# Reads of a pair of score banks given precedence on VectorE and ScalarE in both mixers of a two-layer encoder trunk

## The chip, the cores and the metric

The kernel runs on one core of one Trainium2 chip. The metric is device time in microseconds (us) of one execution, the median of several. The engines are named as in the profile: PE is TensorE (matmuls; PEld its weight loads), DVE is VectorE, ACT is ScalarE, POOL is GpSimd, SP is SyncE, which issues the DMAs.

## The reference

Two layers over 1024 tokens of width 1024, all in float32. Layer 0 mixes tokens with two groups of heads side by side: eight heads of latent attention (MLA) and eight of stick-breaking attention. Layer 1 mixes them with sixteen heads of attention over a band of chunks with a learned bias. After each mixer comes a SwiGLU feed-forward part, around all of them RMS norms and residuals. Cut to the parts of the change:

```python
# MLA, per block of 128 queries
s_a = einsum(q_a[blk], k_a[:kend]) * scale_a
p_a = softmax(where(chunk_ok, s_a, -inf))
# stick-breaking, per block of 128 queries
z = einsum(q_b[blk], k_b[:kend]) * scale_b
log_keep = where(before, log_sigmoid(-z), 0)
log_between = cumsum(log_keep, reverse=True) - log_keep
w_b = where(before, exp(log_sigmoid(z) + log_between), 0)
# chunk band: own chunk and the 8 before it
p = softmax(where(valid, einsum(q, k_band) + bias, -inf))
```

## The kernel before

Every large matmul is made of three with float32 operands that are rounded to a shorter form and a rest: high by high, high by low, low by high (lines 287 to 289 in `mm3`). So each weight that comes from memory (`wr`) is split: `wh` is its rounded form, `wl` the rest, one instruction each of 128x512 (lines 250, 252 and 255 in `round_to` and `rest`). Which engine does a split is written out per weight. Activations are split in the same way (`u`, `c`).

PSUM, into which PE writes, is cut into three sets: two single banks `mm` for projections, two single banks `o` for outputs, and two *pairs* of banks `z`. A pair holds a tile of scores for two heads (128 x 2 x 512 at most). Whoever takes a pair waits until the one that had it two takes ago has been read. All attention goes through these two pairs:

- Stick-breaking (`sb_step`): for each tile of 128 keys by up to 512 queries and two heads, four matmuls give scores `z` (lines 901, 902); DVE clamps them into `a` (904), which frees the pair. ACT does Exp and Ln (905, 906), DVE a maximum (907), ACT and then DVE and POOL (one head each) split the result into `c` (911, 255). A later stage takes another pair and sums along the keys by matmuls with a triangle (923, 926, 928). ACT and DVE carry the last row on to the next tile (930, 931); DVE subtracts the sums from `a` (934), which frees that pair, and ACT does the exponential (935). The last stage multiplies with the values (838 in `weighted`).
- MLA: `mla_max` makes scores (1056) and takes row maxima `m` (1058) on DVE; they are gathered (1038) and transposed on PE (1040), and go negated into the queries (1042). `mla_attend` makes the scores again (1127 to 1129), ACT takes the exponential out of the pair (1130). `soft_step` divides by the sum (1095 to 1101).
- Band: `band_max` adds the bias and takes the maximum in one instruction per head (1185), `band_attend` adds the bias (1210) and takes the exponential (1211).

`step` runs the three stages of a tile with a distance of `LAG` = 2 tiles between them. `weave` mixes the attention of one pair of heads with *fill*: the projections of the next pair, which need only weights and so can run while attention waits. In the stick-breaking part fill is `sb_project` (the next heads' queries and keys) and values; with the last pair of heads, `prepare` (MLA's latent projections, their norms at 310 and 323 to 327, rotary embedding at 995 to 997).

What sets the order: inside the mixers a scheduler of the framework puts the instructions of each engine in a queue. It takes what is ready, by rank, and the rank is the place in the program. Once it is set, each engine works through its queue in order and waits at the first instruction that is not ready. The feed-forward parts are pinned to the order of the program.

## Time and profile before

| | us |
|---|---|
| three runs, median (lowest to highest) | 2587.18 (2587.08 to 2593.2) |
| the profiled execution | 2588.75 |
| its span, first to last instruction | 2586.6 |
| PE busy from 660 to 1340 us (feed-forward of layer 0, projections of layer 1) | 669.23 of 680 |
| PE busy from 1880 us on (end of layer 1) | 683.41 of 707 |

A row of the page or of a group names the line, the engine, the operation and its tiles with their shapes. Behind the bar stand the busy time, the mean duration of one in ns, and the idle time of the engine just before them with what ended it. A row of the waits names the waiting instruction, what it waited for, the total, the number of times and the longest.

### The profile page before, as it was taken

Reading aid. Unit: us, or ns where it says so; the run is one execution under the profiler, and the core shown is the slowest. Engines: PE = TensorE matmul, PEld = TensorE weight load, DVE = VectorE, ACT = ScalarE, POOL = GpSimd, SP = SyncE. Lnnn points to the kernel's source line nnn. Section 1 sums busy time; section 2 is a strip of 40 time slices with the busy share of each in tenths; the row PEclk is TensorE's granted clock in tenths of the full one; section 3 lists DMA queues with packets and bytes.
Section 4 is the critical chain, followed back from the end, with each engine's and each line's share of the span. In section 5 each row is a group of like instructions: output and inputs, shape, how many; then the busy total and the mean of one; then the engine's idle time right before and its main releaser. Section 6 shows DMA issues by size and latency. Waiting matters only on the chain.

```text
span 2586.6 us, 33550 instructions
## 1 busy us (share of the span) xinstructions
PE 2508.9 (97%) x11710; PEld 1935.2 (75%) x11710; DVE 1897.3 (73%) x3074; ACT 1168.5 (45%) x2028; POOL 515.5 (20%) x489
## 2 busy tenths in 40 slices
PE   7999998999999999999999999999999999999997
PEld 6766765557778888888878777776777888888886
DVE  6888887666787666677765777777778766667776
ACT  4677676444444344443352343334445443443324
POOL 3333324663000000000031333335300000000004
PEclk9999999999999999999999999999999999999999
DMA  4221100115524343475651222222543434447661
GB/s 139 62 64 54 54 17 29 31 58 163 171 90 151 122 147 133 144 265 193 235 181 54 88 74 83 77 70 90 176 166 102 163 106 142 143 138 261 212 227 70
DMA packets 179432, 319.70 MB, mean 124 GB/s; under 512 B 20544, under 2 KB 36800, under 8 KB 179264
## 3 DMA queue, kind: packets, MB, share of 16 engines
q1 hardware_dynamic: 179264, 317.56, 36.9%
q8 instruction: 93, 1.52, 0.2%
q14 instruction: 75, 0.61, 0.1%
HBM read 222.58 MB, written 84.41 MB: 119 GB/s over the span
## 4 chain that ended last, share of the span: by engine, by line
PE 72%; DVE 9%; DMA 2%; ACT 2%; issue 1%; POOL 0%; DVEq 0%; SPq 0%; POOLq 0%; ACTq 0%
PE z L74 24%; PE mm L74 12%; PE o L74 6%; PE mm L287 6%; PE mm L289 6%; PE mm L288 6%; PE o L838 4%; DVE u L74 2%; PE z L1208 2%; PE z L1182 1%; PE z L1209 1%; PE z L1095 1%; DVE u L310 1%; PE z L1127 1%; DMA wr<-in_w_down 1%
## 5 line engine op out<-in xcount | busy, mean ns | idle before, releaser
L74 PE MATMUL z<-u,wh 128*128 128x512 f32 x976 | 302.2, 390 | 6.4 <-DVE u L74 6.4
L74 PE MATMUL z<-u,vh 128*128 128x512 f32 x976 | 301.7, 390 | 2.8 <-DVE u L74 2.8
L287 PE MATMUL mm<-u,wh 128*128 128x512 f32 x720 | 291.6, 405 | 2.9 <-DVE c L996 1.8
L289 PE MATMUL mm<-u,wl 128*128 128x512 f32 x720 | 284.0, 394 | 0.0
L288 PE MATMUL mm<-u,wh 128*128 128x512 f32 x720 | 283.9, 394 | 0.0
L255 POOL TENSOR_TENSOR wl<-wr,wh 128x512 fp32r<-128x512 f32 (+2 forms) x95 | 122.8, 1297 | 804.3 <-ACT wh L250 732.9
L74 PE MATMUL mm<-u,wh 128*128 128x512 f32 x720 | 224.6, 393 | 3.7 <-ACT wh L74 3.7
L74 PEld LDWEIGHTS z<-u,wh 128*128 128x128 f32 x976 | 183.2, 188 | 47.2 <-DVE u L74 9.4
L74 PEld LDWEIGHTS z<-u,vh 128*128 128x128 f32 x976 | 182.9, 188 | 43.0 <-ACT u L74 4.4
L74 PE MATMUL z<-u,wl 128*128 128x512 f32 x488 | 190.0, 389 | 0.5 <-DVE wl L74 0.5
L74 PE MATMUL z<-u,vl 128*128 128x512 f32 x488 | 189.9, 389 | 0.0
L287 PEld LDWEIGHTS mm<-u,wh 128*128 128x128 f32 x720 | 135.5, 188 | 63.0 <-issue 39.0
L838 PE MATMUL o<-a,u 128*64 128x512 f32 (+3 forms) x768 | 169.6, 488 | 0.2 <-ACT a L1211 0.2
L74 PEld LDWEIGHTS mm<-u,wh 128*128 128x128 f32 x720 | 135.5, 189 | 34.8 <-ACT wh L74 5.6
L289 PEld LDWEIGHTS mm<-u,wl 128*128 128x128 f32 x720 | 135.5, 188 | 32.6 <-issue 5.4
L288 PEld LDWEIGHTS mm<-u,wh 128*128 128x128 f32 x720 | 135.8, 189 | 28.6 <-issue 5.7
L74 PE MATMUL mm<-u,vh 128*128 128x512 f32 x496 | 152.7, 389 | 0.0
L255 POOL TENSOR_TENSOR u<-wr,u 128x512 fp32r<-128x512 f32 x8 | 10.9, 1373 | 667.5 <-ACT u L250 667.5
L74 PE MATMUL mm<-u,wl 128*128 128x512 f32 x360 | 141.2, 392 | 0.7 <-DVE wl L74 0.5
L1211 ACT ACTIVATE a<-a 128x1024 f32<-128x1024 f32 (+3 forms) x96 | 70.5, 738 | 145.1 <-DVE a L1210 144.9
L74 ACT CAST vh<-vr 128x512 fp32r<-128x512 f32 (+1 forms) x166 | 95.9, 577 | 81.5 <-DVE vr L74 31.5
L1079 POOL TENSOR_TENSOR b<-b,a 128x512 f32<-128x512 f32 (+3 forms) x80 | 108.0, 1350 | 114.0 <-ACT a L1211 100.0
(249 smaller groups left out, 5937.7 us busy)
## 6 DMA issues: line engine op xcount, KB each, us to landing
u<-f_t SPq DMA_DIRECT2D x144, 256.0 KB, 5.0
vr<-in_w_up SPq DMA_DIRECT2D x88, 256.0 KB, 4.4
wr<-in_w_gate SPq DMA_DIRECT2D x88, 256.0 KB, 3.6
f_t<-x SPq DMA_DIRECT2D x72, 256.0 KB, 2.0
wr<-in_w_out SPq DMA_DIRECT2D x64, 256.0 KB, 3.0
f_t<-e SPq DMA_DIRECT2D x54, 256.0 KB, 3.6
ld<-f SPq DMA_DIRECT2D x54, 256.0 KB, 5.1
h<-u SPq DMA_DIRECT2D x48, 256.0 KB, 2.5
```

What stands on the lines that cost most here:

```text
L74: return lambda *a, **k: self.tc.keep_in_program_order(f(*a, **k))
L255: self.eng(eng).tensor_tensor(lo, src, hi.bitcast(F32), ALU.subtract)
L287: mm(out, wh, xh, start=first, stop=False, skip_group_check=onto)
L288: mm(out, wh, xl, start=False, stop=False, skip_group_check=onto)
L289: mm(out, wl, xh, start=False, stop=last, skip_group_check=onto)
L310: self.eng(eng).tensor_tensor(acc, acc, sq, ALU.add)
L838: self.nc.tensor.matmul(o[rh, cs], vt[j // 4][:, j % 4, rh], w[:, e, cs], start=first, stop=last)
L1079: self.eng("dve" if dest[2] else "pool").tensor_tensor(st["esum"][:, :, cs], old[:, :, cs], ex[:, :, cs], ALU.add)
L1095: nc.tensor.matmul(den[64 * e:64 * e + 64, :], self.ones[:, 0:64], esum[:, e, :], start=True, stop=True)
L1127: mm(z[:, e, cs], kth[0:kr, bs], qh[0:kr, cs], start=True, stop=False)
L1208: mm(z[:, e, cs], ks[e][kh][0][:, bs], qs[e][hf][0][:, cs], start=True, stop=False)
L1211: nc.scalar.activation(ex[:, :, cs], ex[:, :, cs], AF.Exp)
```

## The change

Seven instructions that read a pair of score banks (and the exponential behind the band's addition) are put in a block that raises their rank by 100 places. Nothing else is touched: each engine has the same instructions as before, in another order.

```diff
+URGENT = 100
...
+    def urgent(self):
+
+        return self.tc.high_priority(offset=URGENT)
...
             zc, t = self.tmp("a"), self.tmp("b")
-            nc.vector.tensor_scalar(zc[:, :, cs], z[:, :, cs], ZMAX, None, ALU.min)
+            with self.urgent():
+                nc.vector.tensor_scalar(zc[:, :, cs], z[:, :, cs], ZMAX, None, ALU.min)
...
             w = x["zc"]
-            nc.vector.tensor_tensor(w[:, :, cs], w[:, :, cs], b[:, :, cs], ALU.subtract)
+            with self.urgent():
+                nc.vector.tensor_tensor(w[:, :, cs], w[:, :, cs], b[:, :, cs], ALU.subtract)
...
-                nc.vector.reduce_max(m2[:, :, r, kh], z[:, :, :n], axis=AX.X)
+                with self.urgent():
+                    nc.vector.reduce_max(m2[:, :, r, kh], z[:, :, :n], axis=AX.X)
...
-                nc.scalar.activation(ex[:, :, cs], z[:, :, cs], AF.Exp, scale=96 ** -0.5)
+                with self.urgent():
+                    nc.scalar.activation(ex[:, :, cs], z[:, :, cs], AF.Exp, scale=96 ** -0.5)
...
-                for e in range(2):
-                    nc.vector.tensor_tensor_reduce(out=z[:, e, :n], in0=z[:, e, :n], in1=tq[:, e, y0:y0 + n],
-                                                   op0=ALU.add, op1=ALU.max, scale=1.0, scalar=-3.0e38,
-                                                   accum_out=m2[:, e, r, kh:kh + 1])
+                with self.urgent():
+                    for e in range(2):
+                        nc.vector.tensor_tensor_reduce(out=z[:, e, :n], in0=z[:, e, :n], in1=tq[:, e, y0:y0 + n],
+                                                       op0=ALU.add, op1=ALU.max, scale=1.0, scalar=-3.0e38,
+                                                       accum_out=m2[:, e, r, kh:kh + 1])
...
-                nc.vector.tensor_tensor(ex[:, :, cs], z[:, :, cs], tk[:, :, xs], ALU.add)
-                nc.scalar.activation(ex[:, :, cs], ex[:, :, cs], AF.Exp)
+                with self.urgent():
+                    nc.vector.tensor_tensor(ex[:, :, cs], z[:, :, cs], tk[:, :, xs], ALU.add)
+                    nc.scalar.activation(ex[:, :, cs], ex[:, :, cs], AF.Exp)
```

The seven are, by the line numbers of before, 904 and 934 (stick-breaking), 1058 and 1130 (MLA), 1185, 1210 and 1211 (band). Line numbers of the changed kernel are 1 to 11 higher. The prediction uses those of before. What moves in the queues is shown at three places. Tiles are named by a letter for their kind and a number that is theirs alone, in both kernels.

**The end of the third pair of heads in stick-breaking** (about 258 to 292 us of before). First DVE. `wl_2731` and `wl_2737` are the rests of a weight of the latent projection, which is fill; `a_2525`, `a_2598`, `a_2657` belong to the last tiles of the third pair of heads, `a_2716` and `a_2769` to the first of the fourth. Before:

```order
L904 TENSOR_SCALAR a_2480<-z_2475 128x1024
L855 SCALAR_TENSOR_TENSOR u_2536<-mm_2449,u_678 128x512
L255 TENSOR_TENSOR wl_2731<-wr_2728,wh_2730 128x512
L255 TENSOR_TENSOR wl_2737<-wr_2734,wh_2736 128x512
L904 TENSOR_SCALAR a_2525<-z_2520 128x1024
```

The changed kernel, some thirty rows further on:

```order
L937 TENSOR_TENSOR b_2354<-z_2700,b_2354 1x1024
L941 TENSOR_TENSOR a_2598<-a_2598,z_2700 128x1024
L941 TENSOR_TENSOR a_2657<-a_2657,z_2755 128x1024
L910 TENSOR_SCALAR a_2769<-z_2764 128x2x256
L997 TENSOR_TENSOR u_2693<-u_2687,u_2693 32x512
L913 TENSOR_TENSOR b_2717<-b_2717,a_2716 128x2x128
L256 TENSOR_TENSOR wl_2731<-wr_2728,wh_2730 128x512
L256 TENSOR_TENSOR wl_2737<-wr_2734,wh_2736 128x512
```

The two rests stand behind the reads of the scores of five more tiles and of the sums of five tiles. Up to L934 of `a_2598` DVE does the same instructions in both, but for the two rests, which are no longer ahead of it, and L904 of `a_2716`, which now is.

On PE, at the same place, `z_2700` and `z_2755` are the sums of the tiles `a_2598` and `a_2657`, and they take the same pair of banks one after the other; `mm_2740` is fill. Before, the last rows ahead of `z_2755`:

```order
L289 MATMUL mm_2740<-u_365,wl_2737 128x512
L287 MATMUL mm_2740<-u_392,wh_2736 128x512
L288 MATMUL mm_2740<-u_393,wh_2736 128x512
L289 MATMUL mm_2740<-u_392,wl_2737 128x512
L923 MATMUL z_2755<-c_2663,masks 128x512 x2
L926 MATMUL z_2755<-b_2354,masks 128x512 x2
L928 MATMUL z_2755<-c_2664,masks 128x512 x2
```

The changed kernel, from the last matmul into `z_2700` to the first into `z_2755`:

```order
L934 MATMUL z_2700<-c_2605,masks 128x512 x2
L906 MATMUL z_2711<-u_2228,u_2437 128x128
L907 MATMUL z_2711<-u_2228,u_2439 128x128
L906 MATMUL z_2711<-u_2229,u_2438 128x128
L907 MATMUL z_2711<-u_2229,u_2440 128x128
L288 MATMUL mm_2740<-u_181,wh_2730 128x512
L289 MATMUL mm_2740<-u_182,wh_2730 128x512
L843 MATMUL o_2459<-a_2525,u_1304 64x512 x2
L929 MATMUL z_2755<-c_2663,masks 128x512 x2
```

Before, all 24 matmuls of `mm_2740` stood ahead of `z_2755`. Now two do; the other 22 stand behind it, from the first that needs `wl_2731` on, which comes right after L838 of `a_2657`.

**The preparation of MLA** (about 380 to 400 us of before), on DVE. `u_3475` and `u_3477` are the norm of the latent queries, `a_3656` a tile of stick-breaking scores, `wl_3588` and `wl_3594` rests of a weight of MLA's values. Before:

```order
L255 TENSOR_TENSOR wl_3588<-wr_3585,wh_3587 128x512
L255 TENSOR_TENSOR wl_3594<-wr_3591,wh_3593 128x512
L931 TENSOR_TENSOR b_3060<-z_3640,b_3060 1x1024
L323 TENSOR_SCALAR u_3570<-o_3568 128x512
L934 TENSOR_TENSOR a_3363<-a_3363,z_3640 128x1024
L325 TENSOR_TENSOR u_3570<-u_3570,u_3572 128x512
L904 TENSOR_SCALAR a_3656<-z_3651 128x1024
```

The changed kernel:

```order
L913 TENSOR_TENSOR b_3509<-b_3509,a_3508 128x1024
L1002 TENSOR_TENSOR f_3531<-mm_3469,u_2562 96x512
L910 TENSOR_SCALAR a_3656<-z_3651 128x1024
L324 TENSOR_SCALAR u_3475<-o_3473 128x512
L256 TENSOR_TENSOR c_3515<-b_3509,c_3514 128x512
L326 TENSOR_TENSOR u_3475<-u_3475,u_3477 128x512
```

L904 of `a_3656`, behind the two rests before, now stands ahead of them and of the norm. It is the one instruction by which the rows up to `wl_3594` differ.

**MLA** (about 546 to 551 us of before), on DVE. `c_4761` is part of the rotary embedding of the next queries; reading `mm_4725` for it frees that bank. Before:

```order
L995 TENSOR_TENSOR c_4760<-mm_4725,u_2562 96x512
L1100 SCALAR_TENSOR_TENSOR f_4663<-z_4660,f_4663 128x512
L1058 TENSOR_REDUCE m_4565<-z_4681 128x2
L1101 TENSOR_TENSOR f_4664<-o_4483,f_4663 128x512
L1058 TENSOR_REDUCE m_4565<-z_4685 128x2
L996 TENSOR_TENSOR c_4761<-mm_4725,u_2562 32x512
```

The changed kernel:

```order
L1002 TENSOR_TENSOR c_4760<-mm_4725,u_2562 96x512
L1066 TENSOR_REDUCE m_4565<-z_4681 128x2
L1108 SCALAR_TENSOR_TENSOR f_4663<-z_4660,f_4663 128x512
L1003 TENSOR_TENSOR c_4761<-mm_4725,u_2562 32x512
L1066 TENSOR_REDUCE m_4565<-z_4685 128x2
L1109 TENSOR_TENSOR f_4664<-o_4483,f_4663 128x512
```

L996 of `c_4761` stands two rows earlier, ahead of the second L1058 and of L1101. At 483 us the rows of DVE are the same in both, at 512 us those of ACT from the cast into `u_4478` on.

In the band the same few rows change places in five of the eight pairs of heads. L1185 of two tiles come to stand among each other, and the scores of one more tile are ahead of a projection's split. Elsewhere the order is that of before.

## The prediction

> **What bounds the kernel now.** First the page: the busy shares and the chain that ended last.
>
> ```profile
> span 2586.6 us, 33550 instructions
> PE 2508.9 (97%) x11710; PEld 1935.2 (75%) x11710; DVE 1897.3 (73%) x3074; ACT 1168.5 (45%) x2028; POOL 515.5 (20%) x489
> PE 72%; DVE 9%; DMA 2%; ACT 2%; issue 1%; POOL 0%; DVEq 0%; SPq 0%; POOLq 0%; ACTq 0%
> ```
>
> TensorE (PE) is busy for 97% of the span; VectorE (DVE) has 9% of the chain. The change touches only the mixers, so next the busy time by stretches. The columns are length, busy time of PE, weight loads, DVE, ACT and POOL, then the granted clock. The stretches are stick-breaking attention (50 to 430 us, with the preparation of MLA at its end), MLA (to 660) and, after a feed-forward part, band attention (1340 to 1880). Two shorter ones follow, from two other questions of the same kind.
>
> ```profile
> 50.00:430.00 380.00, 359.10 (x1694) 258.29 (x1694) 325.96 (x408) 261.11 (x407) 137.42 (x158) 0.98 0.18 51
> 430.00:660.00 230.00, 222.27 (x962) 140.48 (x961) 150.38 (x187) 103.27 (x163) 118.31 (x82) 0.97 0.25 78
> 1340.00:1880.00 540.00, 537.10 (x2857) 391.97 (x2856) 389.71 (x800) 213.58 (x378) 190.41 (x182) 1.00 0.30 92
> ...
> 380.00:400.00 20.00, 13.48 (x45) 8.38 (x43) 18.98 (x25) 14.21 (x29) 7.41 (x5) 0.74 0.13 36
> ...
> 260.00:289.00 29.00, 28.73 (x122) 19.34 (x120) 28.32 (x31) 20.99 (x24) 10.13 (x8) 1.00 0.21 59
> ```
>
> PE is idle for 380 - 359.1 = 20.9, 7.7 and 2.9 us in the three mixers' stretches. **The whole prize is 31.5 us**, and only what the reads of score banks cause of it can be had. In stick-breaking DVE is nearly as full as PE (326 of 380 us), and between 260 and 289 us both are full: 28.3 and 28.7 of 29. There an order can only move waits about, not remove work. What PE waits for there and in MLA (us in total, times, longest):
>
> ```profile
> PE mm L287 <- DVE f L996: 3.1, 1, 3.1
> PE z L928 <- POOL c L255: 2.9, 4, 1.1
> PE z L1040 <- DVE maxes L1038: 2.6, 1, 2.6
> PE o L320 <- DVE u L310: 1.9, 1, 1.9
> PE z L923 <- DVE a L934: 1.4, 3, 0.7
> PE z L901 <- DVE a L904: 1.2, 3, 0.4
> PE z L1056 <- DVE m L1058: 0.9, 1, 0.9
> ```
>
> ```profile
> PE z L1095 <- DVE m L1058: 2.5, 1, 2.5
> PE z L1127 <- ACT a L1130: 1.8, 2, 1.7
> PE mm L287 <- DVE c L996: 1.8, 1, 1.8
> PE z L1056 <- DVE m L1058: 0.9, 2, 0.8
> ```
>
> The first block is 50 to 430 us, the second 430 to 660. Waits that name one of the raised lines sum to 1.4 + 1.2 + 0.9 = 3.5 us in the first and 2.5 + 1.8 + 0.9 = 5.2 us in the second: 8.7 us, a third of a per cent. In the band stretch all idle time is 2.9 us.
>
> **The change part by part.** No instruction is added or taken away; every term is a wait that goes, comes or grows.
>
> *Stick-breaking, the waits that can go.* The raised reads L904 and L934 move up one to five places. Their 1.4 + 1.2 us of waits may all go, and of the 2.9 us on the POOL rest of L255, which ends a chain that begins with L904, I take a third: -3.6 us, between 0 and -5.5 (all three rows).
>
> *Stick-breaking, the wait that comes.* What gives way is the rest of a weight, `wl_2731` and `wl_2737`, now behind the reads of five more blocks (the rows in the section on the change). PE takes its work in order, so the 22 matmuls that need them or stand behind them are now issued after `z_2755`, where before they stood between it and the step that it depends on. PE there now, then DVE, then ACT (start, duration; in brackets the idle time ahead and what ended it):
>
> ```profile
> 284.90 1.08 PE L838 MATMUL o<-a,u 128*64 128x512 f32 x4
> 285.91 0.50 PE L287 MATMUL mm<-u,wh 128*128 128x512 f32 x1
> ...
> 286.71 0.40 PE L287 MATMUL mm<-u,wh 128*128 128x512 f32 x1
> 286.94 0.39 PE L288 MATMUL mm<-u,wh 128*128 128x512 f32 x1
> ...
> 289.15 0.70 PE L923 MATMUL z<-c,masks 128*128 128x512 f32 x2 [0.22 <-DVE a L934]
> ```
>
> ```profile
> 284.95 1.22 DVE L931 TENSOR_TENSOR b<-z,b 1x1024 fp32r<-1x1024 f32 x1
> ...
> 287.78 1.22 DVE L934 TENSOR_TENSOR a<-a,z 128x1024 f32<-128x1024 f32 x1
> 289.03 0.68 DVE L990 TENSOR_TENSOR u<-u,u 32x512 f32<-32x512 f32 x1
> 289.64 0.41 DVE L904 TENSOR_SCALAR a<-z 128x256 f32<-128x256 f32 x1
> 290.08 0.69 DVE L962 TENSOR_TENSOR u<-mm,u 128x512 f32<-128x512 f32 x1
> 290.69 0.68 DVE L255 TENSOR_TENSOR wl<-wr,wh 128x512 fp32r<-128x512 f32 x1
> ```
>
> ```profile
> 283.18 1.00 ACT L930 CAST b<-z 1x1024 fp32r<-1x1024 f32 x1 [0.37 <-PE z L928]
> ...
> 289.03 1.06 ACT L935 ACTIVATE a<-a 128x1024 f32<-128x1024 f32 x1 [0.64 <-DVE a L934]
> ```
>
> The DVE row at 287.78 is L934 `a_2598`, which frees the banks that `z_2755` takes at 289.15. One matmul starts 0.23 us after the other, so without 22 of them PE arrives 22 x 0.23 = 5.1 us earlier, and 0.2 us of wait stands there already: ready at 283.9. DVE cannot follow: up to this L934 it does the same instructions less two rests (2 x 0.68) plus one L904 (0.41), so it is 0.95 us earlier, at 289.0 - 0.95 = 288.05. **PE waits about 4.1 us** where it waited 0.2. The other end: the 0.68 us in which DVE was idle from 260 to 289 goes too, and DVE comes in ahead by the 2.6 us of waits that vanish earlier while PE does not; then it is 4.1 - 0.7 - 2.6 = 0.8 us. I take 4.1, since a gain upstream moves both engines. Then a small one: between the end of `z_2755` and L838 `a_2657` stand its L934 (1.22) and L935 (1.06), 2.4 us with the handing over; PE has over them the four matmuls of `z_2764` (0.45 by their width) and L838 `a_2598` (285.91 - 284.90 = 1.0), so it waits 1.0 us more. `wl_2731` follows that L934 by 2.45 us on DVE (L904 0.68, L990 0.68, L907 0.41, itself 0.68) and PE comes to it after 2.4 + 1.0, so it is there. The sum is 4.1 + 1.0 - 0.2 = **+4.9 us**. The moved matmuls find no wait to hide later, since PE is full from there to 380 us.
>
> *The clock after it.* Rows of PE around 390 us, after waits of 3.1 and 1.9:
>
> ```profile
> 388.26 0.77 PE L287 MATMUL mm<-wh,u 128*128 128x512 f32 x1 [3.11 <-DVE f L996]
> 390.88 2.04 PE L320 MATMUL o<-u,ones 128*128 128x512 f32 x2 [1.86 <-DVE u L310]
> ...
> 394.08 0.63 PE L288 MATMUL mm<-wl,u 128*128 128x512 f32 x1
> 394.51 0.63 PE L289 MATMUL mm<-wh,u 128*128 128x512 f32 x1
> ```
>
> There matmuls start 0.43 us apart instead of 0.23, and the granted clock of 380 to 400 us is 0.74: 0.26 x 20 = 5.2 us of clock lost, a stretch of 10.4 us at half rate. The wait that comes is longer than each of these. A like stretch behind it, with some 8.5 us filled by matmuls, costs 4.2 us and swallows the small wait of 1.0: +3.2 us. Bounds: 0 (no stretch) and +5.2 (all of it filled). I take +3.2, the row at 390 us being the nearest. The Trainium skill, "TensorE: Matmul & The Clock Gate", section "HAM oscillation — how this bites in real kernels", has idle gaps above about 3.4 us throttle the array to half speed, which speaks against this change; by it, the sum would be without this term as soon as DVE cuts the wait below that. This trace has the half rate after a wait of 3.1 us already, so I lean on the row.
>
> *Other places in stick-breaking.* At four more places (`z_945`, `z_1443`, `z_2117`, `z_2293`) the new order leaves 1.4 to 2.5 us of PE work, counted by rows and widths, between a block's last matmul and the next user of its banks, where the old one left 2.3 to 4.3. The reads between are L930, L931 and L934, 1.0 + 1.22 + 1.22 = 3.4 us for a full block. Each may add 0 to 1.1 us; I take +2, between 0 and +4.4.
>
> *Preparation of MLA, 380 to 400 us.* DVE is busy 18.98 of 20 us there and PE only 13.5: DVE is the bound. Up to `wl_3594`, which releases the next values on PE, one more instruction stands on DVE, L904 `a_3656` (1.2 us, the form of 128x1024 below). **+1.2 us** at most, 0 if PE's earlier work hides it; I take +1.
>
> ```profile
> L904 DVE TENSOR_SCALAR a<-z 128x1024 f32<-128x1024 f32 x24 | 29.2, 1215 | 1.3 <-PE z L902 1.1
> L1058 DVE TENSOR_REDUCE m<-z 128x2 f32<-128x1024 f32 x24 | 29.1, 1221 | 13.2 <-PE z L1056 13.0
> L1101 DVE TENSOR_TENSOR f<-o,f 128x512 f32<-128x512 f32 x24 | 16.5, 688 | 0.5
> L1185 DVE CUSTOM_DVE_ANT_0 z<-z,bias 128x256 f32<-128x256 f32 x48 | 20.7, 435 | 0.6 <-PE z L1182 0.2
> ```
>
> *MLA.* The longest two waits on raised lines stay. Around the 2.5 us on L1058 (483 us) DVE's order is unchanged. Around the 1.7 us on L1130 (512 us) ACT still has the cast into `u_4478` ahead of the exponential. What goes is the 1.8 us on L996 (549 us): L996 `c_4761` stands two rows earlier, past one L1058 and one L1101 (1.22 + 0.69 = 1.9 us). With a few tenths of the 0.9 on L1058 that is **-2 us**, between 0 and -4.
>
> *Band.* All is 2.9 us, so at most that can go. Against it: in five pairs of heads the work between two users of a pair of banks falls from 1.93 to 1.25 us at two places, while the two reads of a 128x256 block take 2 x 0.44. That leaves 0.4 us, if DVE is free. I take 0, between -1 and +4.
>
> *Sum.* -3.6 + 4.9 + 3.2 + 2 + 1 - 2 + 0 = +5.5 us. The profiled execution took 2588.75 us (2.15 around its span); so 2594.3. The median of the three is 2587.18, 1.6 less, so **2592.7 us**, +0.21%. A measurement of this kernel can tell about 0.3% (7.8 us) from no change.
>
> **The rivals.**
> *The order starves PE at more places than one.* Mechanism: a rest of a weight gives way to reads, the fill that should cover the reads is not there, and PE waits for DVE where DVE is full. For it: 98% DVE around 280 us, and the clock's stretch at 390. With the four other places at their upper bound (+4.4 for +2), the full stretch (+5.2 for +3.2), the band at +4 and no third of POOL's waits (+1): 5.5 + 2.4 + 2 + 4 + 1 = +14.9, so 2602 us. It decides slower from the point where one wait beyond that at `z_2755` is long enough for a stretch at half rate. Against it: before has 22 matmuls of slack there and elsewhere most orders keep more work between steps than the reads take.
> *The reads' waits vanish and nothing starves.* DVE arrives ahead at `z_2755` (0.8 + 1.0 - 0.2) and no stretch at half rate comes: -5.5 + 1.6 + 0 + 0 + 0 - 4 - 1 = -8.9, so 2578 us. For it: PE does wait on raised reads, 8.7 us. Against it: 4.2 us of these stand where the order is unchanged, and DVE has no room at 280 us. The Trainium skill, "Perfetto Trace Analysis", section "Matmuls", has independent groups rotate through banks so that their evacuation overlaps the next group's matmuls; it speaks for evacuating early only while such matmuls are left, and at `z_2755` few are.
> *It does nothing:* raised reads were first already, and what moves is covered. True for the band; for all, the sum is within 2 us of 2587.
>
> **How the numbers follow.** My sum (2592.7): 0.50, of which 0.39 within 0.3% of before and 0.11 past its upper line of 2594.9, since two terms of 2 to 3 us are open in it. Nothing at all (2587): 0.08, same. Starved at more places (2602): 0.20, slower. Waits vanish (2578): 0.22, of which 0.18 below the lower line of 2579.4 and 0.04 above it. So faster 0.18, same 0.39 + 0.08 + 0.04 = 0.51, slower 0.11 + 0.20 = 0.31. The range runs from the case of vanished waits, half of which is left out below, to a little past that of starving: 2577 to 2605.
>
> **What would show it.** Right: a wait of PE on L934 of 3 to 4 us near 285 us, PE at half rate some 10 us after it, no wait on L996 near 549, unchanged waits near 483 and 512. Wrong: no wait above 1 us near 285, or DVE with idle time before it; waits on L255's rests of weights elsewhere; a band stretch that grows by more than 4 us.

## The result and the profile after

| | before | changed |
|---|---|---|
| median of six runs, us | 2588.89 (2587.08 to 2593.2) | 2606.74 (2603.27 to 2612.08) |
| span of the profiled execution, us | 2586.6 | 2604.2 |

The changed kernel takes 1.0068 times as long (95% interval 1.0057 to 1.0079): **17.6 us slower**, between 15 and 20. The forecast was 5.5 us more than before (2592.7 us), with a range from 2577 to 2605 us; the median of the changed kernel lies 1.7 us above that range. The busy time of the changed kernel in the stretches of the three mixers, in the columns of before:

```profile
50.00:430.00 380.00, 357.41 (x1684) 257.71 (x1683) 322.96 (x404) 259.64 (x403) 135.53 (x158) 0.98 0.18 50
430.00:660.00 230.00, 217.26 (x939) 137.15 (x938) 158.99 (x184) 103.01 (x161) 117.86 (x83) 0.98 0.25 75
1340.00:1880.00 540.00, 535.00 (x2819) 390.10 (x2817) 387.93 (x795) 213.08 (x377) 194.63 (x184) 1.00 0.29 88
```

These stretches are cut at fixed times, so they hold less of the program than before. They say that PE is idle some 5 us more in MLA, not where the time went. For that the two traces are laid side by side by instruction: for every time of before, how much later (+) or earlier (-) the other kernel has finished on DVE what before had finished by then. Each line gives the least of it over the 12 us up to that time, so that a single moved instruction doesn't show. The columns with other names are the experiments below.

```
until us       changed       only_sb      only_mla     only_band    after_glue  after_finish      after_wl  before_again
     100          -1.0          -0.4          +0.5          -3.2          -1.4          -2.5          -4.3          +0.8
     250          -2.9          -2.3          +0.5          -3.2          -3.7          -4.6          -5.3          +0.9
     300          +1.6          +3.0          +0.5          -3.1          +1.6          +0.7          -4.9          +0.9
     430          +2.2          +2.6          +0.3          -3.5          +1.1          +1.6          +0.9          -0.1
     470          +2.6          -0.7          +0.5          -3.1          -0.4          +2.5          +1.1          +0.5
     540          -4.8          -6.6          -2.8          -7.3          -9.7          -4.9          -6.4          -2.1
     620          +6.8          -6.6          +9.7          -7.3          +1.6          -3.0          +6.7          -2.1
    1340          +8.7          -3.8         +10.6          -7.8          +2.7          -1.2          +6.4          -0.4
    1780         +13.2          -4.1         +10.4          -3.1          -1.5          +3.9         +11.7          -0.3
    1880         +15.4          -4.3         +10.5          -1.0          +1.1          +6.0         +15.7          -0.3
    2580         +17.2          +0.1         +11.4          -0.1          +4.2          +7.1         +16.6          +1.9
```

The first column is the account: 1.9 us won from 100 to 250 us, 4.5 lost to 300, 7.4 won from 470 to 540, **11.6 lost from 540 to 620**, and **6.7 lost in the band**. The 1.9 and 1.8 us in the feed-forward parts (620 to 1340, from 1880 on) lie where no queue differs. From 1880 us on every other column loses too, by 0.9 to 4.4 us, and before_again, in which nothing is changed, by 2.2: the profiled execution of before was a quick one there, and this isn't the change's.

**Near 285 us, as forecast.** The busy time from 262 to 300 us, before and then changed:

```profile
262.00:300.00 38.00, 37.59 (x164) 26.10 (x163) 36.69 (x45) 27.39 (x36) 13.58 (x14) 1.00 0.21 63
```

```profile
262.00:300.00 38.00, 33.96 (x139) 22.29 (x139) 34.28 (x39) 22.05 (x29) 12.32 (x12) 0.96 0.19 58
```

PE of the changed kernel there, and DVE below it:

```profile
277.73 0.72 PE L932 MATMUL z<-b,masks 128*128 128x512 f32 x2 [0.73 <-DVE b L937]
...
282.19 0.70 PE L929 MATMUL z<-c,masks 128*128 128x512 f32 x2 [1.02 <-DVE a L910]
...
285.94 0.73 PE L932 MATMUL z<-b,masks 128*128 128x512 f32 x2 [2.15 <-DVE b L937]
...
288.31 3.10 PE L843 MATMUL o<-a,u 128*64 128x512 f32 x8
```

```profile
281.62 0.42 DVE L910 TENSOR_SCALAR a<-z 128x256 f32<-128x256 f32 x1
282.08 0.70 DVE L1003 TENSOR_TENSOR u<-mm,u 32x512 f32<-32x512 f32 x1
282.81 1.12 DVE L256 TENSOR_TENSOR c<-b,c 128x512 fp32r<-128x512 f32 x1
283.96 0.68 DVE L1004 TENSOR_TENSOR u<-u,u 32x512 f32<-32x512 f32 x1
284.67 1.22 DVE L937 TENSOR_TENSOR b<-z,b 1x1024 fp32r<-1x1024 f32 x1
```

DVE works without a gap; PE waits 0.7, 1.0 and 2.2 us, and the clock of the 38 us falls to 0.96. The place and the cause are those forecast. One detail is not: `z_2755` took the pair that L904 frees, and the longer wait is for the row that is carried over (L931, 937 in the changed kernel), not for L934. That `z_2700` and `z_2755` take the same pair holds for the kernel before alone.

**Near 560 us, not forecast.** The changed kernel's largest waits of PE from 535 to 605 us, and then DVE ahead of them:

```profile
PE z L1063 <- DVE f L1108: 4.6, 1, 4.6
PE z L1047 <- DVE maxes L1045: 2.4, 1, 2.4
```

```profile
551.26 0.69 DVE L1002 TENSOR_TENSOR c<-mm,u 96x512 f32<-96x512 f32 x1
551.96 3.54 DVE L1019 CAST u<-u 32x512 fp32r<-32x512 f32 x1
555.53 0.70 DVE L1003 TENSOR_TENSOR c<-mm,u 32x512 f32<-32x512 f32 x1
556.25 3.00 DVE L1019 CAST u<-u 32x512 fp32r<-32x512 f32 x1
559.28 3.95 DVE L1004 TENSOR_TENSOR c<-c,c 32x512 f32<-32x512 f32 x1
563.27 0.70 DVE L1107 SCALAR_TENSOR_TENSOR z<-z,f 128x512 f32<-128x512 f32 x1
564.00 0.69 DVE L1108 SCALAR_TENSOR_TENSOR f<-z,f 128x512 f32<-128x512 f32 x1
```

The division at the end of a pair of heads (lines 1095 to 1101 of before) also holds a pair of banks `z` until its L1100 has read it, and the change does not raise it. Ahead of it stand three rows of rotary embedding for `c_4964` (L1002 to L1004, 995 to 997 before), which stood behind it before. The section on the change doesn't show this place. Two of DVE's three long rows are casts that it had to do here anyway. Before, the same stretch of DVE was:

```profile
557.13 2.93 DVE L1012 CAST u<-u 32x512 fp32r<-32x512 f32 x2
560.60 0.70 DVE L1099 SCALAR_TENSOR_TENSOR z<-z,f 128x512 f32<-128x512 f32 x1 [0.53 <-ACT f L1098]
561.33 0.69 DVE L1100 SCALAR_TENSOR_TENSOR f<-z,f 128x512 f32<-128x512 f32 x1
```

The next scores (L1063) need that pair, so PE stands for 4.6 us, and a stretch at half rate follows: the granted clock of 535 to 605 us is 0.93 (its row stands with the run that raises the division).

**In the band, not forecast.** L838 multiplies a head's weights with its values into 64 rows of `o`; a tile has two heads, on the two halves of the array. PE around one such pair, before (1477 us) and then changed (1486 us); x4 and x2 are its matmuls, two for each head:

```profile
1476.92 0.65 PE L838 MATMUL o<-a,u 128*64 128x256 f32 x4
1477.50 0.50 PE L287 MATMUL mm<-u,wh 128*128 128x512 f32 x1
```

```profile
1485.90 0.65 PE L843 MATMUL o<-a,u 128*64 128x256 f32 x2
1486.48 0.44 PE L1191 MATMUL z<-u,u 128*128 128x128 f32 x2
1486.85 0.65 PE L843 MATMUL o<-a,u 128*64 128x256 f32 x2
1487.43 0.50 PE L288 MATMUL mm<-u,wh 128*128 128x512 f32 x1
```

Side by side, both heads take 1477.50 - 1476.92 = 0.58 us. With scores (L1191) between them each head takes 0.58 by itself. Ten pairs of the band come apart like this, five of 256 columns and five of 128. Outside the band the order parts three more, one near 125 us and two in MLA near 576 and 588 us; no run prices these alone. Their groups, before and changed:

```profile
L838 PE MATMUL o<-a,u 128*64 128x256 f32 x96 | 16.3, 405 | 0.2 <-ACT a L1211 0.2
L838 PE MATMUL o<-a,u 128*64 128x128 f32 x96 | 10.9, 296 | 0.0
```

```profile
L843 PE MATMUL o<-a,u 128*64 128x256 f32 x96 | 19.5, 404 | 0.2 <-ACT a L1222 0.2
L843 PE MATMUL o<-a,u 128*64 128x128 f32 x96 | 13.0, 297 | 0.4 <-ACT a L1222 0.4
```

With the same count and the same mean, the time that the group holds is 3.2 and 2.1 us longer: what ran side by side now runs one after the other. The Trainium skill, "TensorE: Matmul & The Clock Gate", section "The mechanism" (of part 3), says that matmuls which occupy different tiles of the array run at the same time; the rows agree, as long as nothing stands between the two.

### The profile page after: what moved, and what is told of

It is laid out like the page before. It is cut to its first block, busy times and chain, and to the rows that moved or that the text cites. A ratio compares the mean times of both kernels' runs of the same rounds, so it can differ in the third digit from the quotient of the medians.

```text
span 2604.2 us, 33551 instructions
## 1 busy us (share of the span) xinstructions
PE 2514.5 (97%) x11710; PEld 1938.5 (74%) x11710; DVE 1908.2 (73%) x3074; ACT 1169.1 (45%) x2028; POOL 513.1 (20%) x489
## 4 chain that ended last, share of the span: by engine, by line
PE 71%; DVE 9%; DMA 2%; ACT 2%; issue 1%; POOL 0%; DVEq 0%; SPq 0%; POOLq 0%; ACTq 0%
PE z L75 24%; PE mm L75 12%; PE o L75 6%; PE mm L288 6%; PE mm L289 6%; PE mm L290 6%; PE o L843 4%; DVE u L75 2%; PE z L1218 2%; PE z L1191 1%; PE z L1219 1%; DVE u L311 1%; PE z L1103 1%; PE z L1135 1%; DVE wl L75 1%
## 5 line engine op out<-in xcount | busy, mean ns | idle before, releaser
L256 POOL TENSOR_TENSOR wl<-wr,wh 128x512 fp32r<-128x512 f32 (+2 forms) x95 | 122.2, 1291 | 822.4 <-ACT wh L251 749.6
L843 PE MATMUL o<-a,u 128*64 128x512 f32 (+3 forms) x768 | 177.3, 491 | 0.6 <-ACT a L1222 0.6
L256 POOL TENSOR_TENSOR u<-wr,u 128x512 fp32r<-128x512 f32 x8 | 10.9, 1372 | 669.2 <-ACT u L251 669.2
```

The lines of the kernel that those rows point to most:

```text
L256: self.eng(eng).tensor_tensor(lo, src, hi.bitcast(F32), ALU.subtract)
L843: self.nc.tensor.matmul(o[rh, cs], vt[j // 4][:, j % 4, rh], w[:, e, cs], start=first, stop=last)
```

## The experiments

The differences are in us, (ratio - 1) times 2589; by the same rule the changed kernel is at +17.6. Each is a median of 4 to 12 executions.

| run | against before | ratio (95% interval) |
|---|---|---|
| only_sb | -3.9 | 0.9985 (0.9974 to 0.9997) |
| only_mla | +8.0 | 1.0031 (1.002 to 1.0042) |
| only_band | +10.4 | 1.004 (1.0024 to 1.0055) |
| after_band_pairs | +22 | 1.0086 (1.007 to 1.0101) |
| after_glue | +3.6 | 1.0014 (1.0006 to 1.0023) |
| before_glue | -10.9 | 0.9958 (0.9945 to 0.9972) |
| sb_glue | -8.5 | 0.9967 (0.9954 to 0.998) |
| band_split77 | +76 | 1.0294 (1.0281 to 1.0308) |
| after_finish | +9.1 | 1.0035 (1.0024 to 1.0046) |
| after_wl | +18.4 | 1.0071 (1.0056 to 1.0086) |
| after_all_fixed | -5.4 | 0.9979 (0.9969 to 0.9989) |
| sb_glue_wl | -9.3 | 0.9964 (0.9951 to 0.9976) |
| after_glue_finish | -9.6 | 0.9963 (0.9951 to 0.9975) |
| before_glue_finish | -14.5 | 0.9944 (0.9928 to 0.9959) |

**One mixer's part at a time.** Each has the blocks of two mixers taken out of the changed kernel; for only_sb:

```diff
-                with self.urgent():
-                    nc.vector.reduce_max(m2[:, :, r, kh], z[:, :, :n], axis=AX.X)
+                nc.vector.reduce_max(m2[:, :, r, kh], z[:, :, :n], axis=AX.X)
```

and so for L1130, L1185, L1210 and L1211.

> Only the two reads of stick-breaking (904, 934) are raised, MLA and band as before. Theory (three independent places): the trace of the changed kernel is 2.4 us late at 430 us of before, with PE idle 3.4 us and 1.5 us of clock lost more in 262 to 300 us; nothing else is late. So +2 to +4 us against before, with the same waits on L930/L931's banks near 285 us. Rival (one cause, which the reads of stick-breaking start and which drifts into MLA): most of the 17.6 us, over +10 us. A second rival (the order does not matter, the loss is in the runs): within 1.5 us of before.

> Only the two reads of MLA (1058, 1130) are raised. Theory: from 430 to 660 us the changed kernel loses 4.4 us (2.4 late at 430, 6.8 late at 660), made of a stretch at half rate near 490 us that goes (about -5) and a wait of 4.6 us on L1100 of the division near 563 us with a stretch at half rate behind it (about +10). If MLA stands for itself: +3 to +6 us, with the wait on L1100 there, and the stretch at 490 us gone only if it goes by MLA's own order. If the gain at 490 us came from the shifted stick-breaking part, that stretch stays and the kernel is +9 to +11.

> Only the three reads of the band (1185, 1210, 1211) are raised. Theory (split pairs): in five pairs of heads two L838 of one tile, which lie on two halves of the array and run in the time of one, stand apart in PE's queue; each apart costs its own time once more, 0.58 us at 256 columns and 0.36 at 128, five times 0.94 = 4.7 us, less what PE had idle: +4 to +7 us, all of it between 1340 and 1880 us, with PE busy longer and no wait. Rival (reads that stand among each other make PE wait): PE's idle time in the band grows by 4 us or more over 2.9. Rival (no cost in the band, 15.4 - 8.3 = 7.1 us was scatter): within 1.5 us.

Each loss stays at its place. only_sb loses 5.3 us from 250 to 300 us. only_mla loses 12.5 from 540 to 620, behind the same wait of 4.6 us. only_band loses 6.8 from 1340 to 1880. No loss drifts on or begins elsewhere, and the three medians add up to 14.5 of the 17.6 us. only_mla came out between the two cases that were expected. only_sb ends below before all the same, a miss: from 430 to 540 us it comes 9.2 us ahead. Its new order there puts two pairs of L838 of MLA together again, and its clock from 430 to 660 us is 1.00 instead of 0.97 (more on this in the last part of this section). only_band missed the other way by its median (+10.4); its profiled execution was the fastest of eight, so its trace is no measure of the sum. Within MLA the maxima alone did it: with only L1130 raised, every queue has the rows of before.

**Pairs kept together by rank.** In the band, both L838 are raised by 100 places as well.

```diff
-            self.weighted(st["o"], vt, j, x["ex"], cs, first, last)
+            with (self.urgent() if lag == LAG else ExitStack()):
+                self.weighted(st["o"], vt, j, x["ex"], cs, first, last)
```

> The changed kernel, and in the band the two L838 of a tile are raised by 100 places too, which keeps all of them together in PE's queue: ten pairs that the change split, and four that were split before. Split pairs: -4.7 us for the ten and -2.3 for the four (two of 256 and 128 columns, two of 512 and 384, at 0.45 us per 256 columns), so -5 to -8 us against the changed kernel, +10 to +13 against before. Rival (reads among each other): within 1.5 us of the changed kernel, +16 to +19 against before.

A miss, +22: no pair of the band is apart any more, but L838 now stands so early that PE waits for its exponentials:

```profile
PE o L843 <- ACT a L1223: 7.5, 13, 0.9
```

The run couldn't tell the pairs' price, since it changed two things at once. The next binds only the second to the first, and leaves the first its rank.

**Pairs bound together.**

```diff
-        for e in range(2):
-            rh = slice(64 * e, 64 * e + 64)
-            self.nc.tensor.matmul(o[rh, cs], vt[j // 4][:, j % 4, rh], w[:, e, cs], start=first, stop=last)
+        up = self.nc.tensor.matmul(o[0:64, cs], vt[j // 4][:, j % 4, 0:64], w[:, 0, cs], start=first, stop=last)
+        with self.tc.issue_after(up.ins), self.tc.high_priority(offset=100):
+            self.nc.tensor.matmul(o[64:128, cs], vt[j // 4][:, j % 4, 64:128], w[:, 1, cs], start=first, stop=last)
```

> The changed kernel, with the second L838 of each tile bound right behind the first in PE's queue; the first keeps its rank. No pair is apart any more (13 that the change split, 26 that were split before). Theory (split pairs): in the band the ten pairs cost 19.5 - 16.3 + 13.0 - 10.9 = 5.3 us of PE by the groups of 256 and 128 columns, and four more that were apart before some 2 us; the band stretch is 5 to 8 us shorter than in the changed kernel and there is no new wait on exponentials. In MLA 20 pairs come together, 0 to -10 us, since PE waits there for others. In all -6 to -18 us against the changed kernel, -1 to +11 against before. Rival (not the pairs; the reads among each other): band stretch as in the changed kernel, within 2 us of it.

> The kernel before, with the second L838 of each tile bound right behind the first: 26 pairs that stood apart come together (2 in stick-breaking, 20 in MLA, 4 in the band). Theory (a pair apart costs its time once more): -2 us in the band, -1.5 in stick-breaking, 0 to -10 in MLA: -3 to -13 us against before. Rival (in MLA the second of one tile stands beside the first of the next, which makes up for it): only the -3.5 us of the other two.

> Only the two reads of stick-breaking raised, and the second L838 bound behind the first. Theory: the gain of only_sb (-4) and that of the pairs (-3 to -13) add up: -6 to -15 us against before. Rival (MLA's gain in only_sb came by chance from where its stretches at half rate fell): it goes with the new order, and the sum is that of the pairs alone or less.

after_glue is 14 us faster than the changed kernel. From 1340 to 1780 us it comes 4.2 us forward where the changed kernel fell 4.5 us back: the band's loss up to there is the pairs. What is left from 1780 to 1880 us (2.6, in the changed kernel 2.2) goes with one wait on the maxima, which before doesn't have. It stands in the last pair of heads, where the order differs too, though the section on the change names only five others. Its row in the changed kernel (in after_glue it is 1.8 us):

```profile
1848.47 0.41 PE L1047 MATMUL z<-ident,maxes 128*36 128x128 f32 x2 [1.70 <-DVE maxes L1045]
```

The kernel before gains by it too, 10.9 us: it had 26 pairs apart, 20 of them in MLA. The rival, that in MLA the second of one tile makes up for it by standing beside the first of the next, allowed only 3.5 us. It is right for about half: in PE's queue of before, 22 of the 40 L838 of these pairs stand without a neighbour on the other half. At 1.0 us for each pair of 512 columns (285.91 - 284.90 in the rows of the prediction), these cost some 9 us where 20 pairs would cost 18; with the other six pairs this estimate comes to 13 us. Not all that was measured need be the pairs' own time, since the clock of 470 to 500 us is 1.00 in before_glue and 0.83 in before. sb_glue is no faster than the pairs alone, as its rival said.

**More pairs apart.** The changed kernel with L838 of the band raised by 10 places, which parts 77 pairs that stand together in before; the changed kernel parts ten.

```diff
+            with (self.tc.high_priority(offset=10) if lag == LAG else ExitStack()):
```

> The changed kernel, with L838 of the band raised by 10 places, by which 77 pairs of the band stand apart instead of 10 + 4. They hold 24320 columns; a pair of 512 columns apart costs 1.0 us once more by the trace: 77 pairs cost 24320/512 x 1.0 = 47 us, the ten included, so +40 us against the changed kernel, +55 to +60 against before, all of it in the band as PE busy. Rival (a split costs only the switch between kinds of matmuls, 0.1 to 0.2 us): +8 to +15 us against the changed kernel.

+76 us, 58 more than the changed kernel, where 40 was expected and 8 to 15 by the rival: a pair apart costs its time again. The groups hold:

```profile
L843 PE MATMUL o<-a,u 128*64 128x512 f32 x96 | 46.1, 618 | 0.0
L843 PE MATMUL o<-a,u 128*64 128x384 f32 x96 | 37.9, 512 | 0.0
L843 PE MATMUL o<-a,u 128*64 128x256 f32 x96 | 29.7, 405 | 0.3 <-ACT a L1223 0.3
L843 PE MATMUL o<-a,u 128*64 128x128 f32 x96 | 19.1, 298 | 0.0
```

132.8 us, against 27.0 + 21.6 + 19.5 + 13.0 = 81.1 in the changed kernel (the first two groups are the same in before). That is 51.7 of the 58. The rest lies in the band as well: laid side by side, this kernel falls 61.5 us back from 1340 to 1780 us, 57.0 more than the changed kernel. It isn't waiting, since PE's waits from 1340 to 1960 us of this run sum to 1.4 us; what makes it up stays open.

**The division raised as well.**

```diff
-        nc.scalar.activation(r, den, AF.Ln)
...
+        with self.urgent():
+            nc.scalar.activation(r, den, AF.Ln)
+            nc.scalar.activation(r, r, AF.Exp, scale=-1.0)
+            nc.vector.scalar_tensor_tensor(den, den, -1.0, r, ALU.mult, ALU.mult)
+            nc.vector.scalar_tensor_tensor(r, den, 2.0, r, ALU.add, ALU.mult)
```

> The changed kernel, with the division's own reads of its pair of banks raised as well (1097 to 1100: Ln, Exp and two on DVE). In DVE's queue the division of z_4772 then stands ahead of the three rows of rotary embedding for c_4964 again, as before the change. Theory: the wait of 4.6 us on L1100 near 560 us goes, and the stretch at half rate behind it: -8 to -13 us against the changed kernel, +4 to +10 against before; nothing else moves. Rival (PE would have waited for DVE there anyway, which is stretched by POOL's work: three of its rows took 3.0 to 4.0 us instead of 0.7): the wait moves to the maxima of the next scores (L1058), and no more than 3 us are won.

8.5 us faster than the changed kernel, and by its trace the gain lies from 540 to 620 us, where it loses 1.9 instead of 11.6. The 70 us from 535 to 605, changed and then with the division raised:

```profile
535.00:605.00 70.00, 60.85 (x256) 36.82 (x255) 54.91 (x56) 30.40 (x50) 35.04 (x25) 0.93 0.23 72
```

```profile
535.00:605.00 70.00, 65.53 (x296) 41.99 (x295) 52.97 (x65) 34.45 (x56) 40.96 (x28) 1.00 0.31 96
```

PE has 4.7 us more and the clock is back at 1.00 (0.07 x 70 = 4.9 us). The rival, that DVE would be late whatever the order, falls.

**The rests of weights raised as well**, which gives `wl_2731` its place ahead of the last tiles.

```diff
-            self.split(raw[:, :w], hi[:, :w], lo[:, :w], eng_hi, eng_lo)
+            self.round_to(eng_hi, hi[:, :w], raw[:, :w])
+            with (self.urgent() if eng_lo == "dve" else ExitStack()):
+                self.rest(eng_lo, lo[:, :w], raw[:, :w], hi[:, :w])
```

> The changed kernel, with the rests of weights that DVE makes (L255 wl) raised as well. wl_2731 stands 21 rows earlier in DVE's queue, ahead of the last three tiles of the third pair of heads; but on PE only one of the 22 matmuls comes back ahead of z_2755 by its rows... the first that needs wl_2731 stands before z_2755 again, with eight behind it. Theory: the waits of 0.7 + 1.0 + 2.2 us between 262 and 300 us shrink by half or more, the stretch at half rate there goes: -2 to -6 us against the changed kernel. Rival (DVE is the bound there, whatever the order): within 1.5 us of the changed kernel.

The place is mended: from 250 to 300 us it loses 0.4 us instead of 4.5, the clock from 262 to 300 us is 1.00 again and one wait of 1.3 us is left. Nothing is won in the sum (1.0071 against 1.0068), a miss: from 300 to 430 us it gives 5.8 back, where the changed kernel gave 0.6. Two waits of PE on ACT stand there, of 2.6 us (for a `u`) and 1.7 us (for a `c`), that the changed kernel doesn't have. The loss was moved, not removed.

**The mends together.** after_all_fixed has all three, sb_glue_wl the pairs and the rests with only stick-breaking's reads raised, after_glue_finish the pairs and the division. before_glue_finish has these two mends and none of the raised reads.

> The changed kernel with all three mends: the pairs of L838 bound together, the division's reads raised, the rests of weights raised. Theory (three places, which add up): against the changed kernel -14 for the pairs (measured), -8 to -13 for the division, -2 to -6 for the rests: -8 to -15 us against before, level with the kernel before with bound pairs (-11) or a little under it. Rival (the raised reads gain nothing of their own): no better than -11.

> Only the reads of stick-breaking raised, the pairs bound together and the rests of weights raised. Theory: as the same kernel without the rests (-6.4 against before by medians), less 2 to 6 us for the place at 262 to 300 us: -8 to -13 against before. Rival: the reads of stick-breaking win nothing where nothing starves, and this is level with the pairs alone (-11) at most.

> The changed kernel with the pairs of L838 bound together and the division's reads raised, the rests of weights as in the changed kernel. Theory (places add up): -14 and -8.6 against the changed kernel by medians: -3 to -7 against before, with the place at 262 to 300 us as in the changed kernel (4 to 5 us lost). Rival (the mends share their gain): level with before.

> The kernel before with bound pairs and the division's reads raised, no other reads. Theory (what helps is to end early what holds a pair of banks and is short): the wait on L1100 is not in before, so within 2 us of bound pairs alone, -9 to -13 against before. Rival: the division's rows ahead of others cost as the raised maxima did, over 2 us worse than bound pairs alone.

after_glue_finish is 9.6 us under before, 27 under the changed kernel, and better than the 3 to 7 expected. after_all_fixed, with the rests on top, is at -5.4 where -8 to -15 was expected: a miss, and the intervals overlap, so it isn't shown that the rests cost 4 us. sb_glue_wl is level with sb_glue; the rests win nothing there either. The two mends without the raised reads stand lowest of all, at 2577.0 us against 2591.2 of before in the same runs, a little below the -9 to -13 expected. The intervals of before_glue_finish and after_glue_finish overlap, and so do those of the first and before_glue: that the raised reads cost 5 us even where the pairs and the division are mended fits the 5.3 us that after_glue_finish loses from 250 to 300 us, but these medians alone don't show it.

**The kernel before once more.**

> The kernel before once more, the same rows in every queue. Theory (the stretch at half rate near 490 us falls by chance, not by order): its trace stands off that of before by up to 4 us from 470 us on, either way, with the granted clock of 470 to 500 us other than the 0.74 of 480 to 500 us; nothing else moves by more than 1 us at a time. Rival (that stretch belongs to the order of before): it stands there again, the clock is the same, and the 7 us that the changed kernel gains there are the change's.

It ran once, for its trace (2590.71 us). The granted clock from 470 to 500 us (the last but two figures), in before, in this run, and in only_band, whose queues are those of before up to there:

```profile
470.00:500.00 30.00, 27.45 (x99) 14.40 (x98) 23.03 (x27) 11.23 (x19) 12.24 (x10) 0.83 0.06 16
```

```profile
470.00:500.00 30.00, 27.43 (x105) 14.82 (x103) 23.05 (x27) 11.23 (x19) 12.26 (x10) 0.89 0.06 19
```

```profile
470.00:500.00 30.00, 27.44 (x114) 15.88 (x113) 25.03 (x30) 12.49 (x21) 12.33 (x11) 0.94 0.08 25
```

With the same rows the same wait is followed by 5.1, 3.3 or 1.8 us of lost clock, and from 470 to 540 us these two runs come 2.6 and 4.2 us ahead of before. So the size of this loss varies from execution to execution by some 3 us. before_again and only_band ran on different chips; whether that plays a part isn't shown.

That there is a loss at all is hardly chance. The wait is the one on L1058 near 483 us, and the traces of all runs sort by it. Where it is 2.5 us (before, before_again, only_band, only_mla), the clock of these 30 us was 0.83 to 0.94. Where it is 2.3 us (the five runs with bound pairs and raised reads of stick-breaking), it was 0.89 to 1.00. Where it is 2.1 us (before_glue, before_glue_finish) or 1.5 us (the changed kernel and the other five that raise the reads of stick-breaking without binding pairs), it was 1.00 each time. The raised reads of stick-breaking thus cut this wait by 1.0 us, and in none of the six traces with 1.5 us was there a loss of clock, where all four with 2.5 us had one, of 1.8 to 5.1 us. Runs on one and the same chip sort like this too (only_mla and only_band against only_sb). The reads of MLA cut the wait near 512 us from 1.7 to 1.2 us, in only_mla too. Together that is 3.3 to 6.6 of the 7.4 us that the changed kernel wins there. How reads of stick-breaking shorten a wait in MLA isn't shown.

## Why the prediction was wrong

- *"every term is a wait that goes, comes or grows"*: this sentence is the step that failed first. In the band the order changed how long PE works, without any wait: ten pairs apart, 4.5 us up to 1780 us, shown by after_glue and by the dose of band_split77. The band's term was 0, with +4 as its upper bound; it measured +6.7, the last 2.2 of it at one wait on the maxima.
- *MLA, "-2 us, between 0 and -4"*: the second step that failed. It looked at the waits of before on raised lines, and at what stands around those. The new wait is on a read of a pair that is *not* raised: the division's. What is not raised loses in rank against what is, and, by the rows ahead of it here, against what becomes ready sooner because of it. From 540 to 620 us that cost 11.6 us; only_mla has it, after_finish doesn't. The wait on L996 near 549 us that was to go did go: the changed kernel has no wait on it from 535 to 605 us. The two waits that were to stay did not: near 483 us it is 1.5 us instead of 2.5, near 512 us 1.2 instead of 1.7, and the clock behind the first stayed full. In all MLA (430 to 620 us) came to +4.6 us, 6.6 over its term.
- *The wait that comes at `z_2755`, +4.9, and the clock after it, +3.2*: right in place, cause and kind, too large. From 250 to 300 us it was 4.5 us in all, with 3.9 us of waits in three pieces (0.7, 1.0 and 2.2) and 1.5 us of clock (0.04 x 38); these two sum to more than the 4.5, since before has a few tenths of waits there as well. after_wl shows that the late rest of the weight was the cause.
- *Stick-breaking's other terms, -3.6 + 2*: net -1.6 forecast, -1.9 measured from 100 to 250 us. The match is in part luck. PE's waits there are 4.7 us where they were 4.9, but others: the 2.9 us on POOL's rests all went, not a third, and 2.2 us on the carried row (L937) and 1.4 on rests of weights (L256) came. The last is a sign of being wrong that the prediction names. *Preparation, +1*: +0.6 from 300 to 430 us.
- *The sum* missed by less than its steps: 3.6 us too much at `z_2755` stands against 6.6 too little in MLA and 6.7 in the band.
- *The rival "the order starves PE at more places than one", 2602 us*: nearest in size, and only partly right in kind. Its second place is the division's bank, not a rest of a weight; and most of what the band cost was not starving.
- What no term had is the scatter of the half-rate stretch of before near 490 us, 1.8 to 5.1 us with the same rows. One profiled execution isn't a base to 2 us.

## What to carry to other kernels

Raising the rank of some reads of a shared buffer can make every other holder of that buffer later: before doing so, list all who hold it, down to the short ones, and what the work displaced was covering. Where two matmuls run side by side on halves of the array, look in the new order for pairs that come apart, since this adds to PE's time without a wait in any view, and bind them together (10.9 us here, in the kernel before, with what followed from it). To bind, tie the second to the first; raising both moved the cost into 7.5 us of new waits.

## What the hardware showed unexpectedly

DVE's work on SBUF alone was several times slower while POOL ran. The rows L1019 and L1004 of 3.54, 3.00 and 3.95 us quoted above are the slow ends of these two groups of MLA, in the changed kernel from 440 to 640 us (least, median and greatest duration in ns, then the first and last start):

```profile
L1019 DVE CAST u<-u x8: 411/1453/3539, 475.2 to 556.3; 32x512 fp32r<-32x512 f32 x8
L1004 DVE TENSOR_TENSOR c<-c,c x12: 682/683/3954, 443.0 to 585.8; 32x512 f32<-32x512 f32 x12
```

POOL at that time:

```profile
552.86 2.35 POOL L1087 TENSOR_TENSOR b<-a,a 128x1024 f32<-128x1024 f32 x1
...
556.61 2.36 POOL L1087 TENSOR_TENSOR b<-b,a 128x1024 f32<-128x1024 f32 x1
...
560.36 5.09 POOL L1087 TENSOR_TENSOR b<-b,a 128x1024 f32<-128x1024 f32 x2
```

DVE's three long rows end at 555.50, 559.25 and 563.23 us, the first two 0.3 us after a row of POOL (555.21, 558.97). DVE's rows that read a PSUM bank (`mm`, `z`) kept their 0.7 us at the same time. The Trainium skill, "SBUF — State Buffer", section "SBUF: two separate sides", says that DVE and GpSimd share a pair of ports to SBUF under an exclusive lock. By it a DVE instruction that needs the pair (in a two-port mode, or with two inputs from SBUF) waits for the whole instruction of GpSimd, or GpSimd for it; the rows agree. Standing ahead of the division in DVE's queue, the long rows made it later. No run here took POOL's work away, so the cause of the long rows is argued, not shown.
